# Layer two's inner norm: first-mean subtractions moved from GpSimd to VectorE, squares issued one step later

## The chip, the cores and the metric

The kernel runs on one core of a Trainium2 chip. The metric is the device time of one execution, in microseconds (us). The kernel before takes 853.66 us, the median of three runs (853.16 to 853.9).

## The reference, cut to what matters

The model has two layers on 512 tokens of width 1024. The second is a causal convolution module with memory attention beside it; its branch is a convolution of 31 taps over 1536 channels, then a layer norm over those channels, then silu. The change lies in the first steps of that norm:

```
glu = u * sigmoid(g)                                  # 512 x 1536
y   = depthwise_conv(glu, dw_w, 31 taps) + dw_b
mu  = mean(y, -1);  var = mean((y - mu)**2, -1)
y   = silu((y - mu) * rsqrt(var + EPS) * ln_g + ln_b)
out = concat(y, memory_attention(xq)) * silu(gate)    # then @ w_out, RMSNorm, + x
```

## The kernel before, in words

Channels lie on the 128 partitions, so that `y` is the tile `cy` of 12 channel tiles (`ct` 0 to 11) of 128x512 floats. Each projection runs as 16 chunks of six 512-column matmuls (weights and activations are split into a high and a low part, three products each, L302 to L304). `weave` (a loop over chunks) issues after each chunk the side steps due there, then steps of two queues: `filler` (the convolution's taps, L1138, VectorE) and `behind` (the norm's early steps); `step()` takes them in turn. The order of issue is fixed when the program is written, from counts of chunks, and each engine runs its own instructions strictly in that order. Of two tap chains that run interleaved, each begins with a copy (L1131) of the products that ScalarE (L1122) and GpSimd (L1123) have summed for it beforehand.

The norm takes its mean in two parts. When the taps of tiles 0 to 7 are done, `m0_mean` (L1218) sums them over partitions on TensorE (L1220) and ScalarE writes the mean `m0s` (L1222). Then a step for each tile `ct`, from `behind`, does three things: `shift` (L1208) subtracts `m0s` from the tile in place (L1211), on GpSimd for `ct` 0 to 9 and on VectorE for 10 and 11; `square` (L1213) squares it on ScalarE into one of the five buffers `pr`, which the products of L1122 use too; `gather` (L1180) adds the square on GpSimd to a running sum (L1186, L1188). Tiles 8 and 9 follow later (`late_moments`, with their own sum L1242), and 10 and 11 in `ln_ready` (L1281), which empties both queues first. `ln_sums` then reduces the sums on TensorE (L1293, L1294).

Around these steps lies memory attention for the token tiles 2 and 3: transposes on TensorE (L585) with two copies on ScalarE (L586), a reciprocal on VectorE (L573), the products with V on TensorE (L592), a multiplication on VectorE (L596), and the split of its result (L601 on ScalarE, L605 on VectorE). L1278 evacuates the gate projections on ScalarE. L192 and L199 split a weight unit (ScalarE's high part, then two GpSimd subtractions).

The order of issue from the mean on, as it is written (one tap is one L1138; "step n" is the step of tile n):

```
L1222; step 0; L585, L586 x2, L573, L575 x4; tap; step 1; tap; step 2; product
tap; step 3; product; tap; product; L592, L596 (token tile 1)
step 4; tap; step 5; tap; step 6; product; L601; tap; step 7; L605
L585, L586 x2; 3 taps; product; 8 taps with 3 products and one L192/L199; L592, L596 (token tile 2)
4 taps; product; L1278; L601; 2 taps (last of tiles 8, 9); product; L1278; L605
step 8; L1131, tap; L1278; L592, L596 (token tile 3); step 9; L1131, tap; L1242; tap
L1278; L601; 2 taps; L192/L199; L605; 43 taps with L192/L199 and L1278; 2 last taps
shift and square of tiles 10, 11; two sums L1287, L1288; L1293, L1294
```

In the trace VectorE runs ahead of the steps of GpSimd and ScalarE wherever its own instructions wait for nothing. L573 and the taps beside steps 0 to 3 ran before `m0s` was written.

Of the kernel before, what the change touches and what calls it, by code (L numbers as in the profile page):

```python
# [14 lines left out]
ALU = mybir.AluOpType  # L15
# [15 lines left out]
NB = BW // P  # L31
# [61 lines left out]
def trunk(ctx, tc, x, x_t, mem_t, pos, g_cols, w_mem, post_g, w0, w1, dw_w, dw_b,  # L93
          ln_g, ln_b, c_mask, c_xi, c_zeta, c_inv, c_eye, out):
    nc = tc.nc
# [172 lines left out]
    def step():  # L268
        turns[0] += 1
        if behind and (turns[0] % 2 == 0 or not filler):  # L270
            behind.pop(0)()
        else:
            filler.pop(0)[1]()
# [486 lines left out]
    with tc.tile_pool(name="l0", bufs=1) as lp:  # L760
        def w2(tag, bufs, shape=(P, S)):
            return lp.tile(list(shape), F32, tag=tag, bufs=bufs, name=nm(tag))
# [316 lines left out]
    with tc.tile_pool(name="l1", bufs=1) as lp:  # L1079
# [97 lines left out]
        ln = {}  # L1177

        def gather(key, tile_):

            if key not in ln:
                ln[key] = tile_
                return
            if key + "s" not in ln:
                ln[key + "s"] = w2("sum", 1)
                nc.gpsimd.tensor_tensor(out=ln[key + "s"], in0=ln[key], in1=tile_, op=ALU.add)  # L1186
                return
            nc.gpsimd.tensor_tensor(out=ln[key + "s"], in0=ln[key + "s"], in1=tile_, op=ALU.add)  # L1188
# [18 lines left out]

        def shift(ct):  # L1208
            z = cy[:, ct, :]
            eng = nc.gpsimd if ct < NB - 2 else nc.vector  # L1210
            eng.tensor_tensor(out=z, in0=z, in1=ln["m0s"], op=ALU.subtract)  # L1211

        def square(ct):  # L1213
            sq = w2("pr", PR)
            nc.scalar.activation(out=sq, in_=cy[:, ct, :], func=AF.Square)
            return sq

        def m0_mean():  # L1218
            m0 = tp_ps()
            nc.tensor.matmul(m0, ones, ln["ysums"], start=True, stop=True)  # L1220
            ln["m0s"] = w2("m0", 1)
            nc.scalar.mul(out=ln["m0s"], in_=m0, mul=1.0 / (NM * P))  # L1222
            ln["sq"] = []
            for ct in range(NM):
                moments(ct)
            if 4 in summed:
                late_moments()

        def moments(ct):
            def go():  # L1230
                shift(ct)
                gather("dsum", square(ct))
            behind.append(go)

        def late_moments():
            moments(NM)
            moments(NM + 1)
            behind.append(late_mean)
# [42 lines left out]
        def ln_ready():  # L1281
            while filler or behind:
                step()
            for ct in (NB - 2, NB - 1):
                shift(ct)
                ln["sq"].append(square(ct))
            nc.vector.tensor_tensor(out=ln["d2"], in0=cy[:, NB - 2, :], in1=ln["d2"], op=ALU.add)  # L1287
            nc.vector.tensor_tensor(out=ln["d2"], in0=cy[:, NB - 1, :], in1=ln["d2"], op=ALU.add)  # L1288
# [64 lines left out]
        def norm_of(a, b):  # L1353


            steps_ = [(LN[1], ln_ready), (LN[2], ln_sums), (LN[3], ln_cols), (LN[4], ln_spread)]
            for i in range(NB):
                at = LN[4] + 1 + 2 * i
                steps_ += [(at + n, lambda f=f, i=i: f(i)) for n, f in enumerate((z_norm, z_act, z_gate))]
                steps_.append((max(49 + i, at + 3), lambda i=i: z_split(i)))  # L1360
            return [(pos_ - a, fn) for pos_, fn in sorted(steps_, key=lambda s: s[0]) if a <= pos_ < b]
# [81 lines left out]
```

## Time and profile before

| | |
|---|---|
| three runs, median | 853.66 us |
| the profiled execution | 852.9 us |
| its span, first to last instruction | 851.1 us |
| TensorE, share of the span busy | 95% |
| VectorE / ScalarE / GpSimd | 58% / 42% / 52% |
| mean granted TensorE clock | 0.983 |

PE is TensorE's matmul row, DVE is VectorE, ACT is ScalarE, POOL is GpSimd. Times in the rows are us from the span's start. A timeline row merges instructions of one line that follow each other; its duration is from the first start to the last end. The bracket at its end is the idle time of that engine just before it, and what ended it.

### The profile page before, as it was taken

What the parts mean: (1) busy time and instruction counts of PE and PEld (TensorE: products, weight loads), DVE (VectorE), ACT (ScalarE), POOL (GpSimd) and SP (SyncE); (2) the same over time, 40 slices, a digit from 0 to 9 for tenths busy, and PEclk for the clock granted to TensorE, in tenths of its full rate; (3) what the DMA queues carried; (4) which work ended last, traced back from release to release, by engine and by line L of the source; (5) the groups of instructions that cost most, each with busy time, mean ns of one, the idle gap of its engine ahead of it and who ended that gap; (6) DMA issues with size and microseconds to landing.
All of it is one profiled execution on the core that took longest, in us unless ns stands there. A gap on an engine that the chain in (4) does not pass through costs nothing.

```text
span 851.1 us, 10660 instructions
## 1 busy us (share of the span) xinstructions
PE 806.8 (95%) x3904; PEld 677.3 (80%) x3904; DVE 493.5 (58%) x784; ACT 359.0 (42%) x599; POOL 446.1 (52%) x400
## 2 busy tenths in 40 slices
PE   8999999999999999999999999999988389699997
PEld 8888888888888888888889888888867267388886
DVE  5797111244575532443245789999976189756423
ACT  5853366522122143543234254555656262156411
POOL 1155544477676774111242359969753886249202
PEclk9999999999999999999999999999989789899999
DMA  7633644455326355658633534444322102122612
GB/s 280 236 108 114 211 149 148 136 174 179 139 91 207 103 163 193 226 161 271 223 124 125 201 134 143 141 143 144 134 75 99 49 25 100 49 100 74 247 50 99
DMA packets 43171, 122.74 MB, mean 144 GB/s; under 512 B 4976, under 2 KB 6640, under 8 KB 42864
## 3 DMA queue, kind: packets, MB, share of 16 engines
q1 hardware_dynamic: 42688, 121.86, 42.5%
q8 instruction: 30, 0.49, 0.2%
q10 hardware_dynamic: 432, 0.21, 0.1%
q14 instruction: 21, 0.17, 0.1%
HBM read 98.99 MB, written 23.07 MB: 143 GB/s over the span
## 4 chain that ended last, share of the span: by engine, by line
PE 78%; DVE 9%; ACT 5%; POOL 5%; issue 2%; DMA 1%; POOLq 0%; DVEq 0%; ACTq 0%
PE mm L302 22%; PE mm L303 22%; PE mm L304 22%; DVE acc L1138 6%; POOL part L1123 2%; POOL cy L1211 1%; PE tp L592 1%; PE acc L975 1%; PE tp L550 1%; PE tp L956 1%; PE acc L977 1%; POOL sum L1188 1%; PE acc L302 1%; PE acc L303 1%; PE acc L304 1%
## 5 line engine op out<-in xcount | busy, mean ns | idle before, releaser
L199 POOL TENSOR_TENSOR wlo<-wraw,whi 128x512 fp32r<-128x512 f32 x148 | 192.1, 1322 | 150.6 <-ACT whi L192 147.4
L302 PE MATMUL mm<-big,whi 128*128 128x512 f32 (+1 forms) x608 | 237.1, 390 | 4.4 <-ACT big L1278 2.3
L304 PE MATMUL mm<-big,wlo 128*128 128x512 f32 (+1 forms) x608 | 228.3, 376 | 0.0
L303 PE MATMUL mm<-big,whi 128*128 128x512 f32 (+1 forms) x608 | 228.2, 375 | 0.0
L1138 DVE SCALAR_TENSOR_TENSOR acc<-gl,taps,acc 128x512 f32<-128x512 f32 x278 | 185.9, 750 | 0.4
L304 PE MATMUL mm<-whi,big 128*128 128x512 f32 (+1 forms) x432 | 166.9, 386 | 0.0
L302 PE MATMUL mm<-whi,big 128*128 128x512 f32 (+1 forms) x408 | 162.0, 397 | 0.0
L303 PE MATMUL mm<-wlo,big 128*128 128x512 f32 (+1 forms) x408 | 157.7, 387 | 0.2 <-DVE wlo L196 0.2
L302 PEld LDWEIGHTS mm<-big,whi 128*128 128x128 f32 x608 | 115.9, 191 | 25.1 <-ACT big L1278 3.1
L192 ACT CAST whi<-wraw 128x1024 fp32r<-128x1024 f32 x115 | 119.4, 1047 | 39.0 <-PE mm L304 14.2
L304 PEld LDWEIGHTS mm<-big,wlo 128*128 128x128 f32 x608 | 115.7, 190 | 20.9 <-DVE wlo L189 0.2
L303 PEld LDWEIGHTS mm<-big,whi 128*128 128x128 f32 x608 | 116.0, 191 | 19.1 <-issue 1.0
L229 POOL TENSOR_TENSOR stage<-stage 128x512 f32<-128x512 f32 x36 | 49.2, 1366 | 92.8 <-ACT stage L228 92.8
L304 PEld LDWEIGHTS mm<-whi,big 128*128 128x128 f32 x432 | 81.1, 188 | 16.9
L1123 POOL TENSOR_TENSOR part<-part,pr 128x512 f32<-128x512 f32 x70 | 89.6, 1313 | 9.3 <-ACT pr L1122 9.2
L303 PEld LDWEIGHTS mm<-wlo,big 128*128 128x128 f32 x408 | 76.8, 188 | 15.1 <-DVE wlo L196 0.7
L302 PEld LDWEIGHTS mm<-whi,big 128*128 128x128 f32 x408 | 76.7, 188 | 14.5
L196 DVE TENSOR_TENSOR wlo<-wraw,whi 128x1024 fp32r<-128x1024 f32 x41 | 56.5, 1388 | 43.9 <-ACT whi L192 41.6
L1122 ACT ACTIVATE pr<-gl,taps 128x512 f32<-128x512 f32 x70 | 47.2, 717 | 5.3 <-POOL part L1123 5.3
L228 ACT CAST stage<-stage 128x512 fp32r<-128x512 f32 x36 | 22.3, 620 | 50.3 <-DMA stage<-in_w 29.5
L948 ACT ACTIVATE kz<-tp,zeta 128x384 f32<-128x384 f32 x8 | 4.7, 583 | 77.6 <-PE tp L946 77.6
L592 PE MATMUL tp<-w,mv 128*128 128x128 f32 x128 | 18.8, 310 | 19.5 <-ACT w L586 15.4
(217 smaller groups left out, 881.6 us busy)
## 6 DMA issues: line engine op xcount, KB each, us to landing
wraw<-in_w SPq DMA_DIRECT2D x108, 512.0 KB, 4.1
ahead<-stage SPq DMA_DIRECT2D x36, 512.0 KB, 5.1
stage<-in_w SPq DMA_DIRECT2D x36, 256.0 KB, 5.2
whi<-ahead SPq DMA_DIRECT2D x18, 512.0 KB, 4.3
wlo<-ahead SPq DMA_DIRECT2D x18, 512.0 KB, 6.3
wraw<-in_w_mem SPq DMA_DIRECT2D x7, 512.0 KB, 4.7
big<-in_x_t SPq DMA_DIRECT2D x2, 1024.0 KB, 6.9
o<-in_x SPq DMA_DIRECT2D x1, 2048.0 KB, 8.5
```

The lines of the kernel that those rows point to most:

```text
L192: nc.scalar.copy(out=hi, in_=raw)
L196: nc.vector.tensor_tensor(out=lo, in0=raw, in1=hi.bitcast(F32), op=ALU.subtract)
L199: nc.gpsimd.tensor_tensor(out=lo[:, k], in0=raw[:, k], in1=hi[:, k].bitcast(F32), op=ALU.subtract)
L228: nc.scalar.copy(out=st[:, 1].bitcast(F32R), in_=st[:, 0])
L229: nc.gpsimd.tensor_tensor(out=st[:, 0], in0=st[:, 0], in1=st[:, 1], op=ALU.subtract)
L302: nc.tensor.matmul(dst, lh, rh, start=start, stop=False)
L303: nc.tensor.matmul(dst, lh, rl, start=False, stop=False)
L304: nc.tensor.matmul(dst, ll, rh, start=False, stop=stop)
L592: nc.tensor.matmul(po[:, h * P:(h + 1) * P], mv[:, m, h * P:(h + 1) * P], pT[:, m, h, :], start=m == 0, stop=m == 1)
L1122: nc.scalar.activation(out=pr, in_=gl[:, k:k + S], func=AF.Copy, scale=tap)
L1123: nc.gpsimd.tensor_tensor(out=parts[ct], in0=parts[ct], in1=pr, op=ALU.add)
L1138: nc.vector.scalar_tensor_tensor(out=o, in0=gl[:, k:k + S], scalar=tap, in1=ac, op0=ALU.mult, op1=ALU.add)
```

## The change

All ten GpSimd subtractions become VectorE's. The square and its sum for tile n are no longer issued right behind the subtraction of tile n, but behind that of the next tile; the last one (tile 9) is issued in `ln_ready`, ahead of the subtractions of tiles 10 and 11. The number of steps and their places in the order of issue stay as they are.

```diff
         def shift(ct):
             z = cy[:, ct, :]
-            eng = nc.gpsimd if ct < NB - 2 else nc.vector
-            eng.tensor_tensor(out=z, in0=z, in1=ln["m0s"], op=ALU.subtract)
+            nc.vector.tensor_tensor(out=z, in0=z, in1=ln["m0s"], op=ALU.subtract)
...
+        shifted = []
+
+        def squares_of_shifted():
+            while shifted:
+                gather("dsum", square(shifted.pop(0)))
+
         def moments(ct):
+
             def go():
                 shift(ct)
-                gather("dsum", square(ct))
+                squares_of_shifted()
+                shifted.append(ct)
             behind.append(go)
...
             while filler or behind:
                 step()
+            squares_of_shifted()
             for ct in (NB - 2, NB - 1):
                 shift(ct)
```

## Rows read from the trace of the kernel before

**Rows 1.** The page: span; busy us, share and instructions of the engines.
```profile
span 851.1 us, 10660 instructions
PE 806.8 (95%) x3904; PEld 677.3 (80%) x3904; DVE 493.5 (58%) x784; ACT 359.0 (42%) x599; POOL 446.1 (52%) x400
```

**Rows 2.** Timeline, TensorE: start, duration, engine, line, operation, tiles, count [idle before].
```profile
655.06 1.95 PE L592 MATMUL tp<-w,mv 128*128 128x128 f32 x16
...
682.85 3.38 PE L592 MATMUL tp<-w,mv 128*128 128x128 f32 x16 [15.42 <-ACT w L586]
...
730.58 1.86 PE L1293 MATMUL acc<-sum,ones 128*1 128x512 f32 x2 [8.35 <-DVE cy L1138]
```

**Rows 3.** Waits, ScalarE, 640 to 760: waiter, releaser, total us, times, longest.
```profile
ACT pr L1215 <- POOL cy L1211: 28.6, 9, 4.9
```

**Rows 4.** Timeline, ScalarE, 649 to 683.
```profile
649.78 0.61 ACT L1222 ACTIVATE m<-tp 128x512 f32<-128x512 f32 x1
...
677.94 0.60 ACT L601 CAST big<-big 128x512 fp32r<-128x512 f32 x1
...
682.23 1.05 ACT L586 COPY w<-tp 128x512 f32<-128x512 f32 x2
```

**Rows 5.** Timeline, GpSimd, 649 to 674.
```profile
649.97 2.53 POOL L199 TENSOR_TENSOR wlo<-wraw,whi 128x512 fp32r<-128x512 f32 x2 [19.28 <-ACT whi L192]
...
671.07 1.26 POOL L1188 TENSOR_TENSOR sum<-sum,pr 128x512 f32<-128x512 f32 x1 [0.74 <-ACT pr L1215]
672.28 1.26 POOL L1211 TENSOR_TENSOR cy<-cy,m 128x512 f32<-128x512 f32 x1
```

**Rows 6.** Waits, VectorE, 640 to 760.
```profile
DVE big L605 <- ACT big L601: 20.8, 2, 18.9
...
DVE big L596 <- PE tp L592: 6.7, 1, 6.7
...
DVE acc L1131 <- POOL part L1123: 1.2, 1, 1.2
```

**Rows 7.** Timeline, VectorE, 647 to 733.
```profile
647.58 0.18 DVE L573 RECIPROCAL tiny<-tiny 128x4 f32<-128x4 f32 x1
647.68 2.70 DVE L1138 SCALAR_TENSOR_TENSOR acc<-gl,taps,acc 128x512 f32<-128x512 f32 x4
657.04 0.69 DVE L596 TENSOR_TENSOR big<-tp,big 128x512 f32<-128x512 f32 x1 [6.67 <-PE tp L592]
...
678.58 0.74 DVE L605 TENSOR_TENSOR big<-big,big 128x512 fp32r<-128x512 f32 x1 [18.86 <-ACT big L601]
...
701.48 28.40 DVE L1138 SCALAR_TENSOR_TENSOR acc<-gl,taps,acc 128x512 f32<-128x512 f32 x43
...
731.10 1.28 DVE L1211 TENSOR_TENSOR cy<-cy,m 128x512 f32<-128x512 f32 x2
```

**Rows 8.** Timeline, VectorE and GpSimd, around 691.
```profile
690.21 1.29 POOL L1123 TENSOR_TENSOR part<-part,pr 128x512 f32<-128x512 f32 x1
691.02 1.03 DVE L605 TENSOR_TENSOR big<-big,big 128x512 fp32r<-128x512 f32 x1
691.44 1.76 POOL L1123 TENSOR_TENSOR part<-part,pr 128x512 f32<-128x512 f32 x1
```

**Rows 9.** Timeline, VectorE and GpSimd, around 75 (layer one's rotary tables).
```profile
73.56 1.38 POOL L199 TENSOR_TENSOR wlo<-wraw,whi 128x512 fp32r<-128x512 f32 x1 [7.91 <-ACT whi L192]
73.80 1.42 DVE L836 TENSOR_TENSOR cosT<-q,ra 64x256 f32<-64x256 f32 x1
74.90 1.47 POOL L199 TENSOR_TENSOR wlo<-wraw,whi 128x512 fp32r<-128x512 f32 x1
75.23 1.41 DVE L837 TENSOR_TENSOR sinT<-q,ra 64x256 f32<-64x256 f32 x1
...
80.95 0.42 DVE L837 TENSOR_TENSOR sinT<-q,ra 64x256 f32<-64x256 f32 x1
```

**Rows 10.** Windows: busy us of PE, PEld, DVE, ACT, POOL; clock, DMA share, GB/s.
```profile
722.00:731.00 9.00, 0.65 (x3) 0.09 (x2) 9.00 (x14) 0.00 (x0) 0.34 (x1) 0.76 0.18 58
```

## The prediction

> **What bounds the kernel now.** I read the page first: TensorE is busy 95% of 851.1 us, so whatever is to be won lies in its few gaps [rows 1]. Its timeline has two long ones near the norm: 15.42 us before 682.85, ended by ScalarE's copy L586, and 8.35 us before 730.58, ended by VectorE's last tap [rows 2].
>
> The first gap is a queue. ScalarE waited 28.6 us for GpSimd's subtractions, in nine waits [rows 3]. Each tile costs a loop: subtraction 1.26 us on GpSimd, square on ScalarE, sum 1.26 us on GpSimd, and only then the next subtraction, since GpSimd runs in order and the sum stands ahead of it [rows 5]. The attention copies stand behind these squares in ScalarE's queue, so that L601 starts at 677.94 and L586 at 682.23, though their inputs were long there [rows 4]. Through L601 the same queue holds VectorE: L605 waits 18.86 us, and the taps behind it wait with it [rows 7].
>
> The second gap is what VectorE then owes: 43 taps without a pause from 701.48, the subtractions of tiles 10 and 11 at 731.10 [rows 7], and TensorE with nothing to do [rows 10]. So the end is set by when VectorE gets through its taps; TensorE's first gap counts only through VectorE's waits. After 650.38 VectorE idles 6.7 us (L596), 20.8 (L605, two waits) and 1.2 (L1131): 28.7 us in all [rows 6].
>
> **What goes.** With the subtraction in VectorE's queue and the square one step behind, no square waits for GpSimd any more, except for a free `pr` buffer, of which there are five: a square or product needs the sum of the fifth one before it. I follow that chain below as far as L586; it gets there before TensorE does. So both long waits of VectorE go or are filled.
>
> **What comes, op by op.** An undisturbed subtraction on VectorE takes 0.68 us, two of them 1.28 [rows 7]; a tap in a run 28.40 / 43 = 0.66. But the subtraction reads two tiles in SBUF, and such an operation does not run beside a GpSimd one: L605 started at 691.02 beside a sum that ended at 690.21 + 1.29 = 691.50, and ended at 692.05, so 0.55 after it, while the next sum took 1.76 in place of 1.29 [rows 8]. The taps read their accumulator from PSUM and are not held like that in the run of 43. Where VectorE asks again at once, the two take turns: each 0.42 us operation takes 1.42 us while GpSimd has work [rows 9].
>
> The Trainium skill ("SBUF — State Buffer", section "SBUF: two separate sides") has a rule for this: VectorE with two SBUF inputs and GpSimd need the same pair of ports, the one that starts first keeps it for its whole instruction, and the other is blocked. It speaks against this change, and the rows just named bear it out. It does not say who goes next when both wait; if VectorE kept its place, subtraction 7 with L605 behind it, and L605 with subtraction 8 behind it, would each save a GpSimd operation, 2 x 1.25 = 2.5 us less than my sum. The turns of [rows 9] decide for me.
>
> So VectorE's walk. I take 0.66 for a tap, 0.55 after GpSimd's end for a held subtraction, 2.53 / 2 = 1.26 for a GpSimd operation [rows 5], and 1.70 from one to the next where a subtraction slips in (1.76 less the overlap of starts).
>
> - Subtraction 0 now stands ahead of L573 and four taps and waits for the mean, written at 649.78 + 0.61 = 650.39 [rows 4]. In the kernel before those five ran from 647.58 to 650.38 [rows 7], so VectorE loses 2.8 us here.
> - Subtractions 0 and 1 each wait for one of the two weight operations running from 649.97 [rows 5]: they end at 651.8 and, with L573 and a tap between, 653.5. A tap and subtraction 2 bring 654.8. GpSimd starts its first sum about then, so subtraction 3 ends at 656.7, the fourth tap at 657.3; L596, whose input TensorE delivers at 657.0 as before (655.06 + 1.95, [rows 2]), ends at 657.95.
> - From here GpSimd always has a sum ready, and each subtraction with its tap takes one turn of 1.70: 4 ends at 659.6, 5 at 661.3, 6 at 663.0, 7 at 664.75, and L605 in the same way at 666.45.
> - Eleven taps to 673.75, L596 (its input is there at 669) 674.4, six taps 678.4. L605 and subtraction 8 adjoin each other, two turns: 679.5 and 681.2. L1131, tap, L596: 683.15. Subtraction 9, held by one sum, 684.15; L1131 and four taps 687.5; L605 688.5.
> - From there to the subtractions of tiles 10 and 11 nothing changes: from the first of the 43 taps, 701.48, to 731.10 it is 29.62 us [rows 7]. The first tap now starts at 688.43, so they start at 718.05.
>
> That is 13.05 us before 731.10. As a balance: 28.7 of waits go; 2.8 come for the mean, and 12.9 for ten subtractions with their turns, the rest of the wait for L596 and slower L605.
>
> **What lies beside this walk.** ScalarE: copies L586 of tile 2 at 650.4, L575 after L573 to 653.7, squares 0 and 1 to 654.75, then a square or product whenever VectorE has subtracted or a sum has freed a buffer; square 5 at 661.4, L601 at 662.5 (before VectorE asks at 664.75), square 6 at 663.1, L586 at 663.7. TensorE asks for it at 682.85 - 15.42 = 667.4, so its first gap goes with 3 us to spare, and its slow start with it (the sixteen L592 took 3.38 us against 1.95 earlier [rows 2]). TensorE then waits once for about 2 us for L1278 behind square 8 and reaches L1293 near 705, where it waits for VectorE until 718: 13 us against 8.35. The granted clock of that gap is already between its two levels now, 0.76 on the mean [rows 10], so I charge nothing for its being longer.
>
> GpSimd loses ten operations of 1.26 and gains ten delays of about 0.45. Its sum for L1131 is ready at 679 and 680.7, asked for at 681.2 and 684.1. The weight operations behind L1242 start near 685.5, the first pair ends near 688, and TensorE wants it at 694; SP's loads behind them come earlier too. The last square and its sum, issued in `ln_ready`, have their data from 684 on and finish near 704, hidden under the 43 taps; bare, they would cost 0.63 + 1.26. From L1293 on the order is the old one, and I let it move as a block.
>
> **The sum.** 852.9 for the profiled execution less 13.05 is 839.85. That execution lies 0.76 below the median of three, 853.66, so the median becomes 840.6.
>
> **Bounds.** If no subtraction met a GpSimd operation, the ten would cost 10 x 0.6 = 6.0 and the wait for L596 at 657.0 about 1.2 of what was saved: 28.7 - 2.8 - 6.0 - 1.2 = 18.7, or 835.0. If all thirteen (ten subtractions, three L605) took a full 1.75, that is 22.75 against the 16.0 that the walk has for them: 6.75 more, or 847.4. I take the walk, since every overlapping pair in the rows behaves as it assumes.
>
> **The rivals.**
>
> *Fewer meetings.* GpSimd runs out of sums at times, because ScalarE is late with squares, and VectorE slips through: 835.0 to 838.0. For it: GpSimd waits 0.74 before each sum now [rows 5]. Against it: those waits were for squares behind subtractions, and these go. 15%.
>
> *GpSimd becomes the pace.* The delays push its sums back until L1131 waits for the products, or every turn is full: 843.8 to 847.4. For it: the slack at L1131 is only 2 us in my walk. 17%.
>
> *Slower: the square queue holds anyway.* ScalarE's squares stay ahead of L601 and L586, and now need a `pr` buffer that only GpSimd's delayed sums free. If L586 still came at 682.2, VectorE would wait for L601 until 678 as before, subtractions 0 to 7 would lie in that idle time for nothing, and 8 and 9 would be added with their turns, 1.7 + 1.05: 853.66 + 2.75 = 856.4. It decides from the point where the five sums ahead of square 6 end some 18 us later than the 662.5 of my walk, though they take 7.7 us in it; so 4%.
>
> *It does nothing*, a gain of VectorE that TensorE's 95% takes back: against it, TensorE has 13 us of slack at L1293. 3%.
>
> **Chances.** My walk, 838.0 to 843.8, 59%; the others as given, and 2% below 835.0. Range 835.0 to 847.5. A measurement of this kernel tells about 0.2% from no change; by that bound faster 0.93, same 0.03, slower 0.04.
>
> **What would show it.** After the change: no wait of TensorE for L586 near 667; L601 near 662; the ten new subtractions with a mean well over 0.68 (about 1.2 by the walk), and GpSimd sums between them near 1.7; VectorE waiting about 2.8 us for L1222; L1293 waiting some 13 us for VectorE, and the subtractions of tiles 10 and 11 near 718. A mean of 0.68 would show the turns wrong; a wait of L1131 for L1123 would show the second rival; L605 still waiting for L601 by over 10 us, the third.

## The result, and the profile after

The changed kernel takes 840.57 us (median of four, 840.0 to 841.23) against 853.41 for the kernel before (median of four): ratio 0.9849, 95% interval 0.9832 to 0.9866, a gain of 12.8 us. The profiled execution fell by less: its span is 839.4 us and was 851.1 [rows 1], 11.7 less. Line numbers have moved: L1210 is the subtraction (L1211 before), L1214 the square, L1221 the mean, L1285 the gate evacuation, L1301 and L1302 the sums on TensorE (L1293, L1294), L1307 the first VectorE step behind them (L1299).

TensorE's waits of the kernel after, 640 to 760 (waiter, releaser, total us, times, longest). The 15.4 us for L586 [rows 2] are gone, the wait for VectorE has grown from 8.35 to 13.3:

```profile
PE acc L1301 <- DVE cy L1138: 13.3, 1, 13.3
...
PE mm L302 <- ACT big L1285: 1.7, 1, 1.7
```

VectorE's waits in the same stretch. L605, L596 and L1131, 28.7 us together before [rows 6], are no longer among them; the wait for the mean is new, 2.5 us:

```profile
DVE cy L1346 <- ACT cy L1340: 10.7, 8, 4.5
...
DVE cy L1210 <- ACT m L1221: 2.5, 1, 2.5
```

VectorE's timeline after. L605, with [rows 7] at 678.58, now starts at 664.77, and the 43 taps at 688.58 in place of 701.48:

```profile
650.60 1.36 DVE L1210 TENSOR_TENSOR cy<-cy,m 128x512 f32<-128x512 f32 x1 [2.46 <-ACT m L1221]
...
657.99 1.76 DVE L1210 TENSOR_TENSOR cy<-cy,m 128x512 f32<-128x512 f32 x1
...
664.77 1.78 DVE L605 TENSOR_TENSOR big<-big,big 128x512 fp32r<-128x512 f32 x1
...
679.40 1.77 DVE L1210 TENSOR_TENSOR cy<-cy,m 128x512 f32<-128x512 f32 x1
...
688.58 28.39 DVE L1138 SCALAR_TENSOR_TENSOR acc<-gl,taps,acc 128x512 f32<-128x512 f32 x43
...
718.21 1.28 DVE L1210 TENSOR_TENSOR cy<-cy,m 128x512 f32<-128x512 f32 x2
...
724.93 0.68 DVE L1307 SCALAR_TENSOR_TENSOR pr<-tp,m 1x512 f32<-1x512 f32 x1 [4.11 <-ACT m L1306]
```

ScalarE after: the two copies of [rows 4], then at 677.94 and 682.23, now at once behind the squares.

```profile
662.68 0.60 ACT L601 CAST big<-big 128x512 fp32r<-128x512 f32 x1
...
663.77 1.06 ACT L586 COPY w<-tp 128x512 f32<-128x512 f32 x2
```

GpSimd after, sums between subtractions: 1.7 where VectorE slips in, against 1.26 in [rows 5].

```profile
656.21 1.75 POOL L1123 TENSOR_TENSOR part<-part,pr 128x512 f32<-128x512 f32 x1
657.91 1.29 POOL L1188 TENSOR_TENSOR sum<-sum,pr 128x512 f32<-128x512 f32 x1
659.16 3.43 POOL L1123 TENSOR_TENSOR part<-part,pr 128x512 f32<-128x512 f32 x2
```

TensorE behind its wait, first the kernel before, then after. The four L1293 behind the first two took 2.34 us; as L1301 they take 3.29 now, and start 1.73 us behind the subtractions of tiles 10 and 11, not 1.40, since ScalarE's squares come later, 1.05 us behind and not 0.71:

```profile
732.50 2.34 PE L1293 MATMUL acc<-pr,ones 128*1 128x512 f32 x4
...
731.81 1.23 ACT L1215 ACTIVATE pr<-cy 128x512 f32<-128x512 f32 x2 [12.09 <-DVE cy L1211]
```
```profile
717.77 1.86 PE L1301 MATMUL acc<-sum,ones 128*1 128x512 f32 x2 [13.26 <-DVE cy L1138]
719.94 3.29 PE L1301 MATMUL acc<-pr,ones 128*1 128x512 f32 x4 [0.30 <-ACT pr L1214]
...
719.26 1.15 ACT L1214 ACTIVATE pr<-cy 128x512 f32<-128x512 f32 x2 [16.72 <-DVE cy L1210]
```

### The profile page after: what moved, and what is told of

It reads as the page before. It is cut to its first block, busy times and chain, and to the rows that moved or that the text cites. A ratio compares the mean times of both kernels' runs of the same rounds, so it can differ in the third digit from the quotient of the medians.

```text
span 839.4 us, 10668 instructions
## 1 busy us (share of the span) xinstructions
PE 805.0 (96%) x3904; PEld 675.2 (80%) x3904; DVE 507.5 (60%) x794; ACT 359.6 (43%) x599; POOL 437.0 (52%) x390
## 4 chain that ended last, share of the span: by engine, by line
PE 78%; DVE 15%; ACT 4%; issue 2%; POOL 1%; DMA 0%; POOLq 0%; DVEq 0%; ACTq 0%
PE mm L304 22%; PE mm L302 22%; PE mm L303 22%; DVE acc L1138 8%; DVE cy L1210 1%; PE tp L592 1%; PE acc L975 1%; PE tp L550 1%; PE tp L956 1%; PE acc L977 1%; PE acc L302 1%; PE acc L303 1%; PE acc L304 1%; PE tp L933 1%; ACT w L563 1%
## 5 line engine op out<-in xcount | busy, mean ns | idle before, releaser
L1096 ACT ACTIVATE gl<-mm 128x512 f32<-128x512 f32 x12 | 7.2, 600 | 48.6 <-PE mm L304 48.6
```

## The experiments

Eleven kernels were run; an edit is shown against the changed kernel. The question was which of the two edits does the work, whether the turns between VectorE and GpSimd are what a subtraction costs, and what the longer wait of TensorE costs.

**The move alone.** Squares right behind their own subtractions again:

```diff
-                squares_of_shifted()
-                shifted.append(ct)
+                gather("dsum", square(ct))
```

> The ten subtractions on VectorE, each square right behind its own subtraction as in the kernel before. Theory (the move alone breaks the loop, since a square then waits for VectorE and not for a GpSimd queue that holds the sums): the same 13 us less than before but for about 1 us, 840 to 843, TensorE's wait for L586 near 667 gone or under 2 us, since square 7 now stands ahead of that copy and its subtraction ends at 664.8. Rival (the one-step delay is what lets ScalarE's queue run): a wait of TensorE for L586 of over 5 us and 846 or more.

840.74 us, ratio 0.9854 (0.9839 to 0.9869): the whole gain. TensorE does not wait for L586; it waits 5.2 us for the gate evacuations, hidden under what is left of its wait for VectorE:

```profile
PE acc L1292 <- DVE cy L1138: 8.0, 1, 8.0
PE mm L302 <- ACT big L1277: 5.2, 2, 2.8
```

**The delay alone.** Subtractions on GpSimd as before, squares one step later:

```diff
-            nc.vector.tensor_tensor(out=z, in0=z, in1=ln["m0s"], op=ALU.subtract)
+            eng = nc.gpsimd if ct < NB - 2 else nc.vector
+            eng.tensor_tensor(out=z, in0=z, in1=ln["m0s"], op=ALU.subtract)
```

> The ten subtractions stay on GpSimd, each square is issued one step later, behind the next tile's subtraction. Theory (the loss before was that each sum stood between two subtractions in GpSimd's queue and waited for the square; one step later it waits for nothing): GpSimd runs without gaps, reaches subtraction 6 near 670 and not 680.4, TensorE's wait for L586 shrinks from 15.4 to about 4 us, L605 comes about 8 us earlier, and VectorE, which gets no new work, ends some 10 us earlier: 842 to 845. Rival (GpSimd is too slow for subtractions and sums whatever the order): 849 to 853.

856.17 us, ratio 1.0027 (1.0017 to 1.0038): slower than before, which neither theory had. The first half of the theory held: GpSimd ran without gaps, TensorE waited 3.7 us for L586, and L605 asked at 669.93, 8.7 us earlier than before. But then it stood for 14.8 us, here VectorE's and GpSimd's timelines:

```profile
669.93 14.82 DVE L605 TENSOR_TENSOR big<-big,big 128x512 fp32r<-128x512 f32 x1 [9.57 <-ACT big L601]
```
```profile
669.29 1.28 POOL L1211 TENSOR_TENSOR cy<-cy,m 128x512 f32<-128x512 f32 x1
670.51 1.29 POOL L1188 TENSOR_TENSOR sum<-sum,pr 128x512 f32<-128x512 f32 x1
671.74 1.29 POOL L1123 TENSOR_TENSOR part<-part,pr 128x512 f32<-128x512 f32 x1
...
680.40 3.80 POOL L1123 TENSOR_TENSOR part<-part,pr 128x512 f32<-128x512 f32 x3
694.01 1.28 POOL L1123 TENSOR_TENSOR part<-part,pr 128x512 f32<-128x512 f32 x1 [9.81 <-ACT pr L1122]
```

GpSimd passed it eleven times, each operation at its usual 1.3 us. GpSimd's run ended at 684.20 and L605 at 684.75, the same 0.55 behind GpSimd's end as in [rows 8]: it had been blocked all along. So the turns are not a law; the next three runs, all with the delay alone, ask what this hold costs.

**Delay alone, with L605 of token tile 1 on GpSimd.**

```diff
-            nc.vector.tensor_tensor(out=yx[1][:, :, tok], in0=gx[:, :, tok],
-                                    in1=yx[0][:, :, tok].bitcast(F32), op=ALU.subtract)
+            eng = nc.gpsimd if rs is None and t == 1 else nc.vector
+            eng.tensor_tensor(out=yx[1][:, :, tok], in0=gx[:, :, tok],
+                              in1=yx[0][:, :, tok].bitcast(F32), op=ALU.subtract)
```

> As the kernel with the delay alone (subtractions on GpSimd, squares one step later), but token tile 1's L605 is done by GpSimd and not by VectorE. In the run with the delay alone that L605 stood on VectorE for 14.8 us, from 669.93 until GpSimd had nothing left. Theory (that one blocked instruction, and what waits behind it, is the whole reason why the delay alone was slower): without it VectorE's taps run on, waiting some 6 us for attention and some 6 us for GpSimd's products; the subtractions of tiles 10 and 11 come near 720 and not 734; 842 to 846. Rival (GpSimd is the pace in any case): 850 or more.

850.38 us, ratio 0.9959 (0.9947 to 0.9971): faster than before, but on the rival's side and not as the theory had it. The trace does not show GpSimd as the pace, though: the next such operation, token tile 2's (L606 here), was held in the same way, and the subtractions of tiles 10 and 11 came at 727.50:

```profile
679.12 12.05 DVE L606 TENSOR_TENSOR big<-big,big 128x512 fp32r<-128x512 f32 x1
```

**Delay alone, L605 asking later.** A dead operation (nothing reads its result) with one operand in PSUM stands ahead of it:

```diff
+            if rs is None and t == 1:
+                other = [*accs.values()][-1].rearrange("p (h n) -> p h n", h=XH)
+                nc.vector.tensor_tensor(out=yx[1][:, :, tok], in0=yx[0][:, :, tok].bitcast(F32),
+                                        in1=other, op=ALU.subtract)
```

> As the kernel with the delay alone, with one more VectorE operation right ahead of token tile 1's L605: the same form with one operand in PSUM, its result overwritten by L605 (a dead result). It waits for the same copy L601, so that L605 asks some 0.6 us later. Theory A (the 14.8 us are an accident of when L605 asks): it is held for at most one GpSimd operation, 1.8 us, and the time falls to 842 to 846. Theory B (what GpSimd has queued decides, and it has eleven operations whose inputs are all there): L605 is held as before until GpSimd runs out, and the time stays at 855 to 857.

856.14 us, ratio 1.0022 (1.0012 to 1.0032). L605 (L609 here) asked 0.73 us after the dead operation and was held for 14.09, until GpSimd ran out; the dead operation, with one operand in PSUM, took 0.69 in the middle of GpSimd's run:

```profile
668.00 0.69 DVE L607 TENSOR_TENSOR big<-big,acc 128x512 fp32r<-128x512 f32 x1 [9.57 <-ACT big L601]
668.73 14.09 DVE L609 TENSOR_TENSOR big<-big,big 128x512 fp32r<-128x512 f32 x1
```

This speaks against A, though it moves the asking only once. Why a queue of ready operations should decide, as B has it, it does not show.

**Delay alone, all three later L605 on GpSimd** (`t > 0` in place of `t == 1`).

> As the kernel with the delay alone, with L605 of all three later token tiles on GpSimd. With tile 1's alone there, the next L605 was held 12.05 us. Theory (a VectorE operation with two SBUF inputs that loses its turn to a GpSimd queue with all inputs there is the whole of what made the delay alone slow): no VectorE operation between 650 and 730 takes over 2 us, VectorE still waits for GpSimd's products at L1131, now behind two more operations, and the subtractions of tiles 10 and 11 come near 722; 843 to 847. Rival (GpSimd is the pace): 849 or more.

842.63 us, ratio 0.9866 (0.9852 to 0.988), just under the range. No VectorE operation is held any more; the subtractions of tiles 10 and 11 come at 720.40, and VectorE waits for GpSimd's products as expected:

```profile
DVE big L596 <- PE tp L592: 13.7, 2, 7.0
...
DVE acc L1132 <- POOL part L1124: 6.3, 1, 6.3
```

From 856.17 to 842.63, 13.5 us, and the subtractions of tiles 10 and 11 from 734.04 to 720.40, by three operations: the held L605 was the reason why the delay alone was slow. So the delay mends the same loop as the move, and nearly as well once no L605 can be held.

**One SBUF input.** In the changed kernel, tiles 1 to 9 subtract the running accumulator in PSUM, not the mean (this kernel leaves the mean out of them, so its output is not the norm's):

```diff
+            other = [*accs.values()][-1] if 0 < ct < NB - 2 else ln["m0s"]
-            nc.vector.tensor_tensor(out=z, in0=z, in1=ln["m0s"], op=ALU.subtract)
+            nc.vector.tensor_tensor(out=z, in0=z, in1=other, op=ALU.subtract)
```

> As the changed kernel, but the subtractions of tiles 1 to 9 take the running convolution accumulator, which lies in PSUM, in place of the mean, which lies in SBUF (so the mean is left out of these tiles): the same operation, form and count on VectorE, with one SBUF input. Theory (the turns with GpSimd are what makes a subtraction cost 1.2 us): each takes 0.68, the GpSimd sums between them 1.26 and not 1.7, and the subtractions of tiles 10 and 11 come 3.5 to 5.5 us earlier; 835 to 837.5. Rival (a subtraction costs that much anyway, or its waits are for data): no change, 840.6.

837.31 us, ratio 0.9816 (0.9803 to 0.983). The same operation beside the same GpSimd sums takes 0.68, and the sums stay at 1.3 (VectorE, then GpSimd):

```profile
658.27 0.68 DVE L1211 TENSOR_TENSOR cy<-cy,acc 128x512 f32<-128x512 f32 x1
...
659.65 0.69 DVE L1211 TENSOR_TENSOR cy<-cy,acc 128x512 f32<-128x512 f32 x1
```
```profile
657.61 1.30 POOL L1188 TENSOR_TENSOR sum<-sum,pr 128x512 f32<-128x512 f32 x1
658.87 2.54 POOL L1123 TENSOR_TENSOR part<-part,pr 128x512 f32<-128x512 f32 x2
```

The subtractions of tiles 10 and 11 start at 715.16 and not 718.21, 3.05 us earlier, a little under the 3.5 expected: VectorE then waits 1.0 us for L596, and L605 still takes its turns. The Trainium skill ("SBUF — State Buffer", section "SBUF: two separate sides") has it that a VectorE operation with two SBUF inputs and a GpSimd operation block each other; the traces agree, with 1.24 us on the mean for a subtraction with two SBUF inputs beside GpSimd's work and 0.68 with one. The rule says nothing of who goes next, and the delay alone shows that it can be GpSimd eleven times over.

**The wait filled with dead work.** Eleven matmuls ahead of L1301, then sixteen:

```diff
-            es, vr = tp_ps(), acc_ps()
+            es = tp_ps()
+            for _ in range(11):      # then 16
+                nc.tensor.matmul(es, ones, cy[:, 0, :], start=True, stop=True)
+            vr = acc_ps()
```

> As the changed kernel, with eleven matmuls of a dead result (ones against tile 0, about 1.1 us each, so some 12 us) issued on TensorE in its wait for VectorE ahead of L1301; they write the buffer that L1302 overwrites. Theory (the wait of 13 us lets the clock fall, and L1301 then runs at the lower level in the chain that sets the end): L1301's six matmuls each take 0.6 and not 1.05, L1307 comes some 2 us earlier, 838 to 839.5. Rival (the clock in this gap costs nothing, as I had charged it): 840.6, or later if the matmuls run past VectorE's end.

840.91 us, 0.9856 (0.9842 to 0.9869), no gain, but the eleven took 9.60 us and left 3.83 idle, in which the clock fell all the same; L1301 (L1304 here) was no faster than before. So this run could not tell the theory from the rival:

```profile
703.85 9.60 PE L1301 MATMUL tp<-cy,ones 128*128 128x512 f32 x22
717.27 1.87 PE L1304 MATMUL acc<-sum,ones 128*1 128x512 f32 x2 [3.83 <-DVE cy L1138]
719.44 3.57 PE L1304 MATMUL acc<-pr,ones 128*1 128x512 f32 x4 [0.30 <-ACT pr L1214]
```

Its stretch from 717 to 720, with the granted clock third from the end of the row (1.00 is the full level, 0.50 the lower one):

```profile
717.00:720.00 3.00, 2.43 (x3) 0.20 (x4) 2.96 (x6) 1.15 (x2) 0.00 (x0) 0.50 0.03 8
```

> As the changed kernel with sixteen dead matmuls in TensorE's wait, not eleven: the eleven took 9.60 us, ended 3.83 us before VectorE, and the clock still fell in what was left. Sixteen take 14.0 us and end within half a microsecond of VectorE's last tap. Theory (the idle time ahead of L1301 is what lowers the clock): L1301's six matmuls take about 0.6 each, L1307 comes 1.5 to 2.3 us earlier than in the changed kernel, 838.2 to 839.2. Rival (the clock's fall costs this chain nothing): 840.6 or a little more.

840.0 us, 0.984 (0.9826 to 0.9854), between the theory's range and the rival's time. In the profile the theory holds: with no idle time ahead, the clock stays at its full level, L1304 takes 1.02 and 1.88 us, and the way from the subtractions of tiles 10 and 11 (717.93) to the first step behind the sums (723.25) is 5.32 us, against 718.21 to 724.93, 6.72, in the changed kernel.

```profile
717.94 1.02 PE L1304 MATMUL acc<-sum,ones 128*1 128x512 f32 x2
719.66 1.88 PE L1304 MATMUL acc<-pr,ones 128*1 128x512 f32 x4 [0.71 <-ACT pr L1214]
```
```profile
717.00:720.00 3.00, 2.29 (x6) 0.35 (x5) 2.96 (x6) 1.02 (x2) 0.00 (x0) 1.00 0.01 3
```

The times do not tell 840.0 from 840.57: the 1.4 us are a reading of two traces, not of the clocked runs.

**The wait filled with useful work.** The norm's sums are issued later, so that chunks of the third gate's projection, work that does not need the norm, stand ahead of the wait (34, 43 and 40 are the chunk at which the sums are issued):

```diff
-LN = (7, 32, 34, 36, 39)
+LN = (7, 32, 43, 45, 48)      # the other run: (7, 32, 40, 42, 45)
```

> As the changed kernel, with the norm's sums issued at chunk 43 and not 34, its columns at 45 and the spread at 48 (before 36 and 39): nine chunks of the third gate, 12.3 us of TensorE work, then stand ahead of the wait for VectorE. Theory (TensorE idles 13.3 us there with useful work behind the wait, and the clock falls in it): the wait shrinks to about 1 us, the clock stays up, and the time falls by 6 to 12 us, to 829 to 835; what it does not give is lost where the output projection then waits for the normalised tiles. Rival (the tiles set the end, whatever TensorE does before): 838 to 841.

> The same with the sums at chunk 40, columns at 42 and spread at 45: six chunks, 8.2 us of TensorE work, ahead of the wait. Theory: the wait shrinks to about 5 us and the time falls by about 8 us, to 831 to 835. Rival (the tiles set the end): 838 to 841.

At 43: 827.81 us, ratio 0.9687 (0.9675 to 0.97), 26 us below the kernel before that ran beside it; this is the fastest of all, and a little under the theory's range. TensorE waits about 1 us for VectorE and the clock is at its full level, 1.00 where it was 0.68 (704 to 718, the changed kernel, then this one):

```profile
704.00:718.00 14.00, 0.74 (x4) 0.21 (x3) 14.00 (x22) 0.00 (x0) 1.85 (x2) 0.68 0.10 37
```
```profile
704.00:718.00 14.00, 12.19 (x52) 9.03 (x50) 14.00 (x23) 0.31 (x1) 0.31 (x1) 1.00 0.11 37
```

At 40: 832.88 us, ratio 0.975 (0.9736 to 0.9765), as expected; TensorE waits 3.1 us for VectorE. In its profile one L605 was held too, for 3.73 us in all:

```profile
677.96 3.73 DVE L605 TENSOR_TENSOR big<-big,big 128x512 fp32r<-128x512 f32 x1
```

Later sums in the kernel before, which also has 8.35 us of such a wait, were not run, so how much of this second gain needs the change is not shown.

**The move alone with the sums at 43.**

> The move alone, without the one-step delay, and the sums at chunk 43. Theory (the delay adds nothing measurable, as the run of the move alone had it): 826 to 829, as with both. Rival (with TensorE's wait filled, ScalarE's queue counts again): 830 or more.

830.24 us, ratio 0.9715 (0.9702 to 0.9728): the rival's side by a little. In the profile TensorE's 3.9 us of waits for the gate evacuations, behind the squares in ScalarE's queue, are no longer under another wait; but that execution took 827.57, on the theory's side, so its trace does not explain the median. The kernel was not timed beside the run with both edits, and the intervals all but touch, so I take it as a sign that the delay is worth some 2 us once the wait is filled, and not as shown.

## Why the prediction was right

The time, 840.57, is the forecast 840.6, and the walk (VectorE's operations one by one) stands almost to the tenth. That the two agree to the tenth is in part luck, as told below.

- *What goes.* Forecast: TensorE's first gap closes with 3 us to spare, L601 at 662.5, L586 at 663.7. Measured: 662.68 and 663.77; no wait.
- *The wait for the mean.* 2.8 forecast, 2.46 measured.
- *The turns.* Subtraction 3 was to end at 656.7, 4 at 659.6, L605 at 666.45, subtraction 8 at 681.2, 9 at 684.15, the 43 taps to begin at 688.43, tiles 10 and 11 at 718.05. Measured: 656.81, 659.75, 666.55, 681.17, 684.23, 688.58, 718.21. The ten subtractions take 1.24 us on the mean (12.4 in all); the run with one SBUF input shows that it is the turns, worth 3.05 us at the end of the taps.
- *TensorE's idle time.* To reach L1293 near 705 and wait 13 us: 704.5 and 13.3.
- *The tail as a block.* From L1299 to the end of the span it was 851.1 - 736.54 = 114.6 us and is 839.4 - 724.93 = 114.5. Ahead of that, from the subtractions of tiles 10 and 11 to L1299, it did not hold.

Two steps were wrong, without much effect on the time. One let everything from L1293 on "move as a block" and charged nothing for the longer idle time. From the subtractions of tiles 10 and 11 to the step behind the sums the kernel before took 736.54 - 731.10 = 5.44 us and the changed one 6.72. Of these 1.28 us, 0.95 lie in the four L1301, which ran longer at the lower clock (the granted clock is 0.65 from 720 to 724, and was 0.92 from 733 to 736 in the kernel before), and 0.33 in the later squares; in all four traces that have both edits and issue the sums where the changed kernel does, the four matmuls start 1.73 or 1.74 us behind the subtractions, in the others with the old place of the sums 1.39 to 1.46. That is why the span of the profiled execution fell by 11.7 and not by the 12.9 that these subtractions came earlier. The other three runs were 0.5 to 1.2 us faster than the profiled one, so that the median came out at the forecast all the same: luck, and not a sum without an error.

The length of the idle time does not set this price. The same way was 6.24 us long behind 16.90 us of idle time (L605 of token tile 1 on GpSimd), 6.72 behind 13.26 (the changed kernel), 5.44 behind 8.35 (the kernel before) and 7.00 behind 3.83 (eleven dead matmuls, 717.71 to 724.71); the nine traces with an idle wait there lie between 5.44 and 7.00, in no order of its length, and the one without at 5.32. Besides the squares, what differs is how many of the six matmuls behind the wait still run at the lower clock; what decides that is open, and the sum had no term for it. The run with 16.90 us (its way is 727.50 to 733.74):

```profile
727.06 1.86 PE L1303 MATMUL acc<-sum,ones 128*1 128x512 f32 x2 [16.90 <-DVE cy L1139]
728.89 3.15 PE L1303 MATMUL acc<-pr,ones 128*1 128x512 f32 x4
```

The other wrong step is the reason I gave for the end of the loop. I named both edits together, and the move alone does it all: once the subtraction is on VectorE, the sum no longer stands between two subtractions, whichever step the square is in. The delay alone does nearly as much where no L605 can be passed over: 842.63.

And "every overlapping pair in the rows behaves as it assumes" was true of the rows and too strong as a rule. Over the thirteen traces, whose programs differ little, a VectorE operation with two SBUF inputs that found GpSimd at work, with GpSimd's next operation following at once, was let in behind the current one well over 200 times, and passed over 4 times, each time until GpSimd ran out. All four are L605, once each in four kernels, none in the changed one. The rival that went slower had the place wrong (ScalarE's queue); the risk that the runs show lay in VectorE's own.

What decides when it is passed over is open. It isn't the moment alone: the four asked 0.14, 0.59, 0.64 and 0.96 us into an operation of GpSimd, while in the changed kernel a subtraction or L605 that asked anywhere from 0.08 to 1.17 us into one was let in, one L605 at 0.64. In the run with sums at 40 it was passed over in the place where the changed kernel's, in the same order of issue, was let in.

## What to carry to other kernels

Where three engines pass one tile round, look at what stands between two turns in each queue: moving one link or issuing it a step later may break the same loop, and one of them can be enough. Count for every VectorE operation with two SBUF inputs beside a busy GpSimd what its turn cost here, 1.1 to 1.8 us, not its own 0.68, and know that it can be far more; give such operations a place where GpSimd has a pause or one operand in PSUM. And when another engine has a wait ahead of a chain's end, look for work that can be moved into it: in the changed kernel that was worth as much as the change itself.

## What was not expected of the hardware

A VectorE operation with two SBUF inputs can be held for 14.8, 14.1, 12.1 and 3.7 us while GpSimd runs from one operation to the next, though the same two engines take turns, one operation each, nearly everywhere else. TensorE's granted clock fell with 3.83 us of idle time left ahead of L1304 and did not fall in that place without any; and the way behind such a wait, 5.44 to 7.00 us, went by something other than the wait's length.
